# Memory attention in one transformer layer: the query and output weights multiplied into keys and values ahead of time

## The chip, the cores and the metric

The kernel runs on one core of one Trainium2 chip. A core has a matrix engine (TensorE, PE in the profile; PEld is its weight load), a vector engine (DVE), a scalar engine (ACT), a general engine (GpSimd, POOL) and an engine that here only issues transfers (SyncE, SP). Each takes its instructions in order and waits for others by semaphores. Matmuls write to PSUM, which the other engines read; the working memory of 128 partitions is SBUF; main memory (HBM, "DRAM" in the code) is reached by DMA. All DMAs of this kernel are issued from SP's one queue, in order.

The metric is the device time of one launch in microseconds. Three runs of the kernel before gave 1541.18, 1542.2 and 1542.79; the median is 1542.2.

## The reference

One layer of a streaming encoder on x of 1024 rows by 1024 columns, with 256 memory rows. The part that the change touches is the second sub-layer:

```python
def memory_cross_attention(h, mem_n, w_mq, w_mk, w_mv, w_mo):
    q = (h @ w_mq).reshape(B, S, MEM_HEADS, MEM_HEAD_DIM)        # 4 heads of 256
    k = (mem_n @ w_mk).reshape(B, M, MEM_HEADS, MEM_HEAD_DIM)    # M = 256 memory rows
    v = (mem_n @ w_mv).reshape(B, M, MEM_HEADS, MEM_HEAD_DIM)
    logits = jnp.einsum('bshd,bmhd->bhsm', q, k).astype(jnp.float32) * (MEM_HEAD_DIM ** -0.5)
    p = jax.nn.softmax(logits, axis=-1).astype(v.dtype)
    o = jnp.einsum('bhsm,bmhd->bshd', p, v).reshape(B, S, D_MODEL)
    return o @ w_mo

# in reference(), after the token mixing has given x:
h = rmsnorm(x, g_mem_pre[l])
mem_n = rmsnorm(mem, g_mem_kv[l])
y = memory_cross_attention(h, mem_n, w_mq[l], w_mk[l], w_mv[l], w_mo[l])
x = x + rmsnorm(y, g_mem_post[l])
h = rmsnorm(x, g_ff_pre[l])
y = jnp.square(jax.nn.relu(h @ w_ff1[l])) @ w_ff2[l]
```

Ahead of it stand two attentions over x (eight heads each: one with forget gates, one over chunks) with an output projection w_out; behind it stands the MLP. Each sub-layer has a norm before and after it.

## The kernel before

All products are kept near fp32. Each operand is split into a high part that TensorE takes (fp32r) and a low part, the rest. One product is then three matmuls: `mm3` (L100) issues high by high (L102), high by low (L103) and low by high (L104). A weight is loaded as 128 x 1024 numbers (512 KB) by `load_w` (L83) into a raw buffer `wraw`, of which there are three. ACT copies it to the high part `whi` (L96), and DVE or POOL subtracts that for the low part `wlo` (L97), two buffers of each. `lo_eng` (L423) gives the subtraction to DVE and POOL by turns in the first phase, and to DVE alone once `quiet` is set after it. Other tiles of 4 KB a partition (activations, row results) come from one pool `u4` of 31 buffers. PSUM has four tags of two banks each: mm, s, tr and pv.

*First phase (up to about 566 us).* Projections and the attention heads alternate; each head writes its output to main memory (`od`, L393). The normalised memory rows are turned (columns of the model on the partitions, `mT`) in `mem_turn`. At the end of the phase `mem_keys` (L431) makes the keys `km`: 8 weights of w_mk, each used by 24 matmuls of 256 columns (matmuls to tiles mk). `mem_values` (L442) makes the values `vm`: 8 weights of w_mv, each used by 12 matmuls of 512 columns (tiles mv). Keys and values stay in SBUF.

*Second phase.* The sequence is half of 512 rows (`th` = 0 or 1) by half. `head_outputs` (L540) loads the attention outputs from `od` into tiles `oin` (L549), splits them into yT_hi (ACT, L552) and yT_lo (DVE, L553) and adds their squares (L556 to L561) for the group norms. `mix_out` (L583) is the output projection (tiles yw): four matmul blocks to a weight, the squares summed by a small product (ssh, L568), the reciprocal root made on DVE and POOL (L569, L570), evictions on ACT for the first group (L605) and DVE for the second (L607). `close_block` (L629) adds the residual row and norms; `turn` (L643) transposes the rows for the next product, h2 for the memory attention and h3 for the MLP.

`cross(th)` (L647) is the memory attention for one half. For each of four heads: two weights of w_mq, each used by 24 matmuls of 512 columns (tiles mq); the query is split into qh and ql; for each block of 128 rows the scores (tiles ms, 256 columns), maximum, exponential, reciprocal, scaling on POOL (L680); transposes (mtr); and the product with the values (tiles mo), split again. `mem_out` (L613) multiplies with w_mo, 8 weights per half, each used by 24 matmuls of 512 columns (tiles ym).

The order of calls: `cross(0)` at L725 with the turns of the second half's h2 between its heads, `mem_out(0)` at L727, `close_block` of half 0, `cross(1)` at L731 with the turn of half 0's result y0 into h3 after its first head, then the POOL sums `xf` of h3's two parts that the MLP's Strassen scheme needs (L855), the first column half of `mem_out(1)` (L857), the loads `wo` of the second column half (L858), and from `residual_in(0)` on an order written out by hand: the second column half of `mem_out(1)` block by block, between its blocks the residual rows, then the MLP. Up to there the framework's scheduler orders the calls' instructions by its own model of their times; each engine then runs the given order.

Of the kernel before, what the change touches and what calls it, by code (L numbers as in the profile page):

```python
# [13 lines left out]
F32 = mybir.dt.float32  # L14
# [30 lines left out]
def build(ctx, tc, nc, out, t):  # L45
# [122 lines left out]
    cd = dr.tile([8, S], F32, name="cd")  # L168

# [261 lines left out]
    def mem_keys(mT):  # L431
        km = Act("km", NM)
        for nb in range(KC):
            wh, wl = load_w(t["w_mk"][nb], [P, KC, P], lo_on=lo_eng())
            ps = mm_tile([P, NM], f"mk{nb}")
            for kc in range(KC):
                mm3(ps, wh[:, kc, :], wl[:, kc, :], mT.hi(kc), mT.lo(kc), kc == 0, kc == KC - 1)
            nc.scalar.activation(km.hi(nb), ps, AF.Copy)
            nc.vector.tensor_sub(km.lo(nb), ps, f(km.hi(nb)))
        return km  # L440

    def mem_values(mT):  # L442
        vh = [u4(f"vm_hi{m}", (P, D)) for m in range(2)]
        vl = [u4(f"vm_lo{m}", (P, D)) for m in range(2)]
        for nh in range(2):
            cs = slice(nh * HT, (nh + 1) * HT)
            ps = [mm_tile([P, HT], f"mv{nh}{m}") for m in range(2)]
            for kp in range(4):
                wh, wl = load_w(row_pair(t["w_mv"], kp, nh), [P, 2, HT], lo_on=lo_eng())
                for m in range(2):  # L450
                    ms = slice(m * P, (m + 1) * P)
                    for j in range(2):
                        kc = kp * 2 + j
                        mm3(ps[m], mT.hi(kc, ms), mT.lo(kc, ms), wh[:, j, :], wl[:, j, :],
                            kc == 0, kc == KC - 1)
            for m in range(2):
                nc.scalar.activation(vh[m][:, cs], ps[m], AF.Copy)
                nc.vector.tensor_sub(vl[m][:, cs], ps[m], f(vh[m][:, cs]))
        return vh, vl
# [69 lines left out]
    km = mem_keys(mT)  # L529
    vmh, vml = mem_values(mT)  # L530
# [82 lines left out]
    def mem_out(th, o, y, ss, g, nhs=(0, 1)):  # L613

        for nh in nhs:
            cs = slice(nh * HT, (nh + 1) * HT)
            ps = [mm_tile([P, HT], f"ym{th}{nh}{b}", "mm" if b < 2 else "s") for b in range(4)]
            for kp in range(4):
                wh, wl = load_w(row_pair(t["w_mo"], kp, nh), [P, 2, HT], lo_on=lo_eng())
                for b in range(4):  # L620
                    c = slice(b * P, (b + 1) * P)
                    for j in range(2):
                        mm3(ps[b], o[kp][0][:, j, c], o[kp][1][:, j, c], wh[:, j, :], wl[:, j, :],
                            kp == 0 and j == 0, kp == 3 and j == 1)
# [22 lines left out]
    def cross(th, act, after=None):  # L647

        out_h = []
        for h in range(4):  # L650
            qh, ql = [], []
            for nb in range(2):
                wh, wl = load_w(t["w_mq"][h * 2 + nb], [P, KC, P], lo_on=lo_eng())
                ps = mm_tile([P, HT], f"mq{th}{h}{nb}")
                for kc in range(KC):
                    mm3(ps, wh[:, kc, :], wl[:, kc, :], act.hi(kc), act.lo(kc), kc == 0, kc == KC - 1)
                a = p2x.tile([P, HT], F32R, tag="qh", bufs=4, name=f"qh{th}{h}{nb}")
                b = p2x.tile([P, HT], F32R, tag="ql", bufs=4, name=f"ql{th}{h}{nb}")
                nc.scalar.activation(a, ps, AF.Copy, scale=0.0625)
                nc.vector.scalar_tensor_tensor(b, ps, 0.0625, f(a), op0=ALU.mult, op1=ALU.subtract)  # L660
                qh.append(a)
                ql.append(b)
            ph = p2x.tile([P, 2, HT], F32R, tag="ph2", bufs=1, name=f"ph{th}{h}")
            pl = p2x.tile([P, 2, HT], F32R, tag="pl2", bufs=1, name=f"pl{th}{h}")
            for b2 in range(2):
                tr = mm_tile([P, 2, 2, P], f"mtr{th}{h}{b2}", "tr")
                for j in range(2):
                    b = b2 * 2 + j
                    bs = slice(b * P, (b + 1) * P)
                    ps = mm_tile([P, NM], f"ms{th}{h}{b}", "s")  # L670
                    for nb in range(2):
                        mm3(ps, qh[nb][:, bs], ql[nb][:, bs], km.hi(h * 2 + nb), km.lo(h * 2 + nb),
                            nb == 0, nb == 1)
                    st = small.tile([P, 3], F32, tag="mst", bufs=4, name=f"mst{th}{h}{b}")
                    pr = p2x.tile([P, NM], F32, tag="mp", bufs=4, name=f"mp{th}{h}{b}")
                    nc.vector.tensor_reduce(st[:, 0:1], ps, axis=mybir.AxisListType.X, op=ALU.max,
                                            negate=True)
# [3 lines left out]
                    for m in range(2):  # L681
                        nc.tensor.transpose(tr[:, m, j, :], pr[:, m * P:(m + 1) * P], ident)
# [707 lines left out]
```

## Time and profile before

The profiled execution took 1547.0 us; its span, from the first to the last instruction, is 1545.2 us at a mean granted clock of 0.995. What is told below of places in time is counted from the start of that span.

| stretch of the span, us | what TensorE does there | PE busy, us |
|---|---|---|
| 0 to 486 | projections, attention | 467.20 of 486 |
| 486 to 528 | attention and memory keys (mk) | 41.90 of 42 |
| 528 to 566 | attention and memory values (mv) | 36.87 of 38 |
| 566 to 668 | output projection (yw), rest of attention | 98.70 of 102 |
| 668 to 741 | memory attention, half 0 | 67.01 of 73 |
| 741 to 796 | mem_out, half 0 | 55.00 of 55 |
| 796 to 893 | memory attention, half 1; first columns of mem_out | 95.85 of 97 |
| 893 to 960 | rest of mem_out, MLP begins | 62.12 of 67 |
| 960 to 1545.2 | MLP | the rest |

A row of instructions in the profile gives line, engine, operation, result and operands by the program's names, the shape and the count; then durations (ns, least, median, most) and the first and last start, or the busy time and the mean. An idle time is put down to what ended it ("<-").

### The profile page before, as it was taken

Reading aid. Unit: us, or ns where it says so; the run is one execution under the profiler, and the core shown is the slowest. Engines: PE = TensorE matmul, PEld = TensorE weight load, DVE = VectorE, ACT = ScalarE, POOL = GpSimd, SP = SyncE. Lnnn points to the kernel's source line nnn. Section 1 sums busy time; section 2 is a strip of 40 time slices with the busy share of each in tenths; the row PEclk is TensorE's granted clock in tenths of the full one; section 3 lists DMA queues with packets and bytes.
Section 4 is the critical chain, followed back from the end, with each engine's and each line's share of the span. In section 5 each row is a group of like instructions: output and inputs, shape, how many; then the busy total and the mean of one; then the engine's idle time right before and its main releaser. Section 6 shows DMA issues by size and latency. Waiting matters only on the chain. (4 is left out here: it accounts for less than half of the span.)

```text
span 1545.2 us, 21983 instructions
## 1 busy us (share of the span) xinstructions
PE 1501.4 (97%) x7852; PEld 1270.6 (82%) x7852; DVE 938.2 (61%) x1640; ACT 789.8 (51%) x1405; POOL 374.2 (24%) x546
## 2 busy tenths in 40 slices
PE   8999999999999999989999998999999999999998
PEld 7978889789878987768888877888888888888886
DVE  6366574665466773775455468676455574746577
ACT  5356564565466675444444455555555544444442
POOL 4234351343234430121011320443233000000021
PEclk9999999999999999999999999999999999999999
DMA  5132140252222454453143154775444595535565
GB/s 215 50 95 66 52 113 23 66 156 64 56 65 90 121 169 139 160 184 106 55 154 105 55 177 168 242 246 181 153 155 150 189 384 194 171 114 192 198 245 191
DMA packets 83856, 220.71 MB, mean 143 GB/s; under 512 B 9865, under 2 KB 13969, under 8 KB 83746
## 3 DMA queue, kind: packets, MB, share of 16 engines
q1 hardware_dynamic: 83746, 219.30, 42.7%
q8 instruction: 62, 1.02, 0.3%
q14 instruction: 48, 0.39, 0.1%
HBM read 159.96 MB, written 50.91 MB: 136 GB/s over the span
## 5 line engine op out<-in xcount | busy, mean ns | idle before, releaser
L96 ACT ACTIVATE whi<-wraw 128x1024 fp32r<-128x1024 f32 x76 | 80.3, 1058 | 76.5 <-PE ym L104 19.0
L1117 ACT ACTIVATE whif<-ra 128x1024 fp32r<-128x1024 f32 x37 | 39.2, 1061 | 122.1 <-PE fy L103 62.6
L1119 DVE TENSOR_TENSOR wlof<-ra,whif 128x1024 fp32r<-128x1024 f32 x37 | 45.3, 1225 | 91.1 <-ACT whif L1117 91.1
L97 DVE TENSOR_TENSOR wlo<-wraw,whi 128x1024 fp32r<-128x1024 f32 x52 | 63.6, 1225 | 53.8 <-ACT whi L96 53.2
L1233 POOL TENSOR_SCALAR rf<-sf 128x1 f32<-128x1 f32 x8 | 8.3, 1035 | 326.5 <-ACT jf L1218 326.2
L102 PE MATMUL v<-whiv,hT_hi 128*128 128x256 f32 (+1 forms) x256 | 73.6, 287 | 1.0 <-DVE vs L235 1.0
L103 PE MATMUL v<-wlov,hT_hi 128*128 128x256 f32 (+1 forms) x256 | 73.2, 286 | 0.0
L104 PE MATMUL v<-whiv,hT_lo 128*128 128x256 f32 (+1 forms) x256 | 73.1, 286 | 0.0
L97 POOL TENSOR_TENSOR wlo<-wraw,whi 128x1024 fp32r<-128x1024 f32 x24 | 57.8, 2410 | 54.2 <-ACT whi L96 28.1
L102 PE MATMUL fx<-vhif,whif 128*128 128x512 f32 x168 | 65.4, 389 | 0.0
L104 PE MATMUL fx<-vhif,wlof 128*128 128x512 f32 x168 | 65.4, 389 | 0.0
L103 PE MATMUL fx<-vlof,whif 128*128 128x512 f32 x168 | 65.4, 389 | 0.0
L1007 POOL TENSOR_TENSOR sc<-wf,wf 128x512 f32<-128x512 f32 x14 | 22.8, 1627 | 144.4 <-DMA wf<-in_w_ff 125.0
L102 PE MATMUL yw<-whi,yT_hi 128*128 128x512 f32 x128 | 51.0, 403 | 2.2 <-ACT yw L605 1.6
L103 PE MATMUL ym<-wlo,oT_hi 128*128 128x512 f32 x128 | 50.9, 397 | 0.9 <-DVE wlo L97 0.8
L103 PE MATMUL mq<-h2T_lo,whi 128*128 128x512 f32 x128 | 51.5, 402 | 0.0
L102 PE MATMUL mq<-h2T_hi,whi 128*128 128x512 f32 x128 | 51.3, 402 | 0.1
L104 PE MATMUL mq<-h2T_hi,wlo 128*128 128x512 f32 x128 | 51.0, 399 | 0.0
L103 PE MATMUL yw<-wlo,yT_hi 128*128 128x512 f32 x128 | 50.6, 395 | 0.1
L102 PEld LDWEIGHTS v<-whiv,hT_hi 128*128 128x128 f32 x256 | 49.1, 192 | 1.5 <-DVE vs L235 1.2
L104 PE MATMUL yw<-whi,yT_lo 128*128 128x512 f32 x128 | 50.3, 393 | 0.0
L104 PE MATMUL ym<-whi,oT_lo 128*128 128x512 f32 x128 | 50.2, 395 | 0.0
(751 smaller groups left out, 5135.5 us busy)
## 6 DMA issues: line engine op xcount, KB each, us to landing
ra<-gd SPq DMA_DIRECT2D x56, 512.0 KB, 3.8
wg<-in_w_ff SPq DMA_DIRECT2D x56, 512.0 KB, 5.6
wf<-in_w_ff SPq DMA_DIRECT2D x38, 512.0 KB, 3.8
gd<-s SPq DMA_DIRECT2D x48, 256.0 KB, 2.1
wraw<-in_w_qk SPq DMA_DIRECT2D x16, 512.0 KB, 4.0
wraw<-in_w_mq SPq DMA_DIRECT2D x16, 512.0 KB, 4.3
wraw<-in_w_mo SPq DMA_DIRECT2D x16, 512.0 KB, 3.8
gd<-u SPq DMA_DIRECT2D x32, 256.0 KB, 2.1
```

The lines of the kernel that those rows point to most:

```text
L96: nc.scalar.activation(hi, raw, AF.Copy)
L97: (lo_on or nc.gpsimd).tensor_sub(lo, raw, f(hi))
L102: nc.tensor.matmul(ps, lh, rh, start=start, stop=False, skip_group_check=more)
L103: nc.tensor.matmul(ps, lh, rl, start=False, stop=False, skip_group_check=more)
L104: nc.tensor.matmul(ps, ll, rh, start=False, stop=stop, skip_group_check=more)
L1007: eng.tensor_sub(sc[:, k1], r0[:, k0], r1[:, k0])
L1117: nc.scalar.activation(ah, ra, AF.Copy)
L1119: nc.vector.tensor_sub(al, ra, f(ah))
L1233: nc.gpsimd.tensor_scalar(r, ssf[b][:, 0:1], ssf[b][:, 1:2], EPS, op0=ALU.add, op1=ALU.add)
```

## The change

The memory attention is regrouped. Before, (h w_mq) k^T p-softmax, times v, times w_mo. After, for each head h the product w_mq k^T (1024 columns of the model by 256 memory rows, scaled by 1/16) and the product v w_mo (256 memory rows by 1024 columns) are made once, at the end of the first phase, and stored to main memory (`kd_d`, `vd_d`, 2 x 4 tiles of 512 KB each). The four heads' folded keys lie side by side as a weight of 1024 by 1024, and so do the folded values.

- `mem_side` makes both keys and values transposed (256 columns a matmul, 24 matmuls a weight). For the values this takes the place of 12 matmuls of 512 columns a weight.
- `fold_keys`: 8 weights of w_mq^T, each used by 24 matmuls of 256 columns; each result is evicted by ACT or DVE into a u4 tile and stored (16 stores of 256 KB).
- `fold_values`: 8 weights of w_mo, each used by 12 matmuls of 512 columns; 8 stores of 512 KB.
- `cross` loads 8 folded key weights per half (as w_mq was before) and makes the scores of two heads and 128 rows in one bank, four banks at a time. There are no queries, no split of them and no product with the values; the transposed probabilities are split at once and are what `mem_out` multiplies.
- `mem_out` loads the folded values in place of w_mo; the squares of a bank are summed before the bank is scaled.
- The order: `cross(1)` follows `cross(0)` at once, ahead of `mem_out(0)`. The second half's h2 is turned in one go after the first two heads of `cross(0)`. The turn of y0 into h3 moves into the first column half of `mem_out(1)`, after its second and third weights, and the loads `wo` go after its fourth. The sums `xf` follow that `mem_out`.
- The host lays w_mq out transposed and w_mv in column blocks.

```diff
+    kd_d = [[dr.tile([P, 2, HT], F32, name=f"wk{kp}_{nh}") for nh in range(2)] for kp in range(4)]
+    vd_d = [[dr.tile([P, 2, HT], F32, name=f"wv{kp}_{nh}") for nh in range(2)] for kp in range(4)]
...
-    def mem_keys(mT):
...
+    def mem_side(mT, src, name):
+        act = Act(name, NM)
         for nb in range(KC):
+            wh, wl = load_w(t[src][nb], [P, KC, P], lo_on=lo_eng())
+            ps = mm_tile([P, NM], f"m{name}{nb}")
             for kc in range(KC):
                 mm3(ps, wh[:, kc, :], wl[:, kc, :], mT.hi(kc), mT.lo(kc), kc == 0, kc == KC - 1)
+            nc.scalar.activation(act.hi(nb), ps, AF.Copy)
+            nc.vector.tensor_sub(act.lo(nb), ps, f(act.hi(nb)))
+        return act
+
+    def fold_keys(km):
+        for h in range(4):
+            for mh in range(2):
+                wh, wl = load_w(row_pair(t["w_mqT"], h, mh), [P, 2, HT], lo_on=lo_eng())
+                for kp in range(2):
+                    ps = mm_tile([P, 2, NM], f"fk{h}{mh}{kp}")
+                    for a in range(2):
+                        c = slice((kp * 2 + a) * P, (kp * 2 + a + 1) * P)
+                        for d in range(2):
+                            mm3(ps[:, a, :], wh[:, d, c], wl[:, d, c], km.hi(h * 2 + d), km.lo(h * 2 + d),
+                                d == 0, d == 1)
+                    g = u4(f"fks{h}{mh}{kp}", (P, 2, NM), F32)
+                    if kp:
+                        nc.vector.tensor_scalar(g, ps, 0.0625, None, op0=ALU.mult)
+                    else:
+                        nc.scalar.activation(g, ps, AF.Copy, scale=0.0625)
+                    nc.sync.dma_start(kd_d[mh * 2 + kp][h // 2][:, :, h % 2 * NM:(h % 2 + 1) * NM], g)
...
-    def mem_values(mT):
...
+    def fold_values(vm):
         for nh in range(2):
+            for h in range(4):
+                wh, wl = load_w(row_pair(t["w_mo"], h, nh), [P, 2, HT], lo_on=lo_eng())
+                g = u4(f"fvs{h}{nh}", (P, 2, HT), F32)
                 for m in range(2):
+                    ps = mm_tile([P, HT], f"fv{h}{nh}{m}")
                     ms = slice(m * P, (m + 1) * P)
+                    for d in range(2):
+                        mm3(ps, vm.hi(h * 2 + d, ms), vm.lo(h * 2 + d, ms), wh[:, d, :], wl[:, d, :],
+                            d == 0, d == 1)
+                    if m:
+                        nc.vector.tensor_copy(g[:, m, :], ps)
+                    else:
+                        nc.scalar.activation(g[:, m, :], ps, AF.Copy)
+                nc.sync.dma_start(vd_d[h][nh], g)
...
-    km = mem_keys(mT)
-    vmh, vml = mem_values(mT)
+    fold_keys(mem_side(mT, "w_mk", "km"))
+    fold_values(mem_side(mT, "w_mv", "vm"))
     p1s.close()
...
+    def mem_out(th, o, y, ss, g, nhs=(0, 1), hook=lambda kp: None):
...
-                wh, wl = load_w(row_pair(t["w_mo"], kp, nh), [P, 2, HT], lo_on=lo_eng())
+                wh, wl = load_w(vd_d[kp][nh], [P, 2, HT], lo_on=lo_eng())
                 for b in range(4):
                     for j in range(2):
+                        mm3(ps[b], *o_at(o, b, kp * 2 + j), wh[:, j, :], wl[:, j, :],
                             kp == 0 and j == 0, kp == 3 and j == 1)
+                hook(kp)
             for b in range(4):
+                square_sum(ps[b], ss[b][:, nh:nh + 1], HT)
                 nc.vector.tensor_tensor(y[b][:, cs], ps[b], g[:, cs], op=ALU.mult)
-                square_sum(ps[b], ss[b][:, nh:nh + 1], HT)
...
     def cross(th, act, after=None):
...
+        o = []
+        for nh in range(2):
+            ps = [mm_tile([P, HT], f"ms{th}{nh}{b}", "mm" if b < 2 else "s") for b in range(4)]
+            for kp in range(4):
+                wh, wl = load_w(kd_d[kp][nh], [P, 2, HT], lo_on=lo_eng())
+                for b in range(4):
+                    c = slice(b * P, (b + 1) * P)
+                    for j in range(2):
+                        mm3(ps[b], act.hi(kp * 2 + j, c), act.lo(kp * 2 + j, c), wh[:, j, :], wl[:, j, :],
+                            kp == 0 and j == 0, kp == 3 and j == 1)
...
+            for b in range(4):
...
+                nc.vector.tensor_reduce(st[:, 0:2], sc, axis=mybir.AxisListType.X, op=ALU.max, negate=True)
+                for h in range(2):
+                    nc.scalar.activation(pr[:, h, :], sc[:, h, :], AF.Exp, bias=st[:, h:h + 1],
+                                         accum_out=st[:, 2 + h:3 + h])
+                nc.vector.reciprocal(st[:, 4:6], st[:, 2:4])
...
+                    nc.gpsimd.tensor_scalar(pr[:, h, :], pr[:, h, :], st[:, 4 + h:5 + h], 1.0,
+                                            op0=ALU.mult, op1=ALU.mult)
                     for m in range(2):
+                        nc.tensor.transpose(tr[:, h * 2 + m, :], pr[:, h, m * P:(m + 1) * P], ident)
...
-    o = cross(0, h2[0], after={0: turn_mixed(1, PAIRS[:1]), 1: turn_mixed(1, PAIRS[1:])})
+    o = cross(0, h2[0], after={0: turn_mixed(1)})
+    o1 = cross(1, h2[1])
     y, ss = y_tiles("m", 0)
     mem_out(0, o, y, ss, gmpost)
     close_block(y, ss, 0, lambda b: x1d[b], lambda b: x2d[b], gffpre, "h3", range(4))
     h3 = [Act("h3T0")]
-    y0 = y
-    o = cross(1, h2[1], after={0: lambda: turn(y0, 0, h3[0], "h3")})
+    y0, o = y, o1
...
+    def meanwhile(kp):
+        if kp in (1, 2):
+            turn(y0, 0, h3[0], "h3", PAIRS[kp - 1:kp])
+        elif kp == 3:
+            wo.extend(load_w(vd_d[k][1], [P, 2, HT], u4, lo_eng()) for k in range(4))
+
+    mem_out(1, o, y, ss, gmpost, (0,), meanwhile)
     for i in range(4):
         for a in range(2):
             xf[i, a] = pr.tile([P, HT], F32, tag="xf", bufs=8, name=f"xf{i}{a}")
...
-    mem_out(1, o, y, ss, gmpost, (0,))
-    wo = [load_w(row_pair(t["w_mo"], kp, 1), [P, 2, HT], u4, lo_eng()) for kp in range(4)]
...
-        "w_mq": blocks(i["w_mq"][0]),
+        "w_mqT": a(i["w_mq"][0].T),
...
-        "w_mv": i["w_mv"][0],
+        "w_mv": blocks(i["w_mv"][0]),
```

The program after, instruction by instruction, has TensorE go through the key fold between the last attention heads, then through 24 matmuls of the key fold, the values' projection and the value fold with no attention work between them, and then to the output projection. In SP's order the load of the first `oin` stands behind two stores of the value fold and one load of a w_out weight.

More of the change, by code (lines that the diff above doesn't have):

```diff
@@ L696, in cross @@
[L696 to L699 removed]
+            if after and nh in after:
+                after[nh]()
+        return o
     gpost = gain(p2, t["g_mix_post"], "g_mix_post")
```

89 lines of the change are left out of this document (15 added, 74 removed).

## The prediction

> **What bounds the kernel now.** I read the page's first part, then the granted clock, then TensorE's waits by releaser, then busy time by stage. The clock, beside the span:
>
> ```profile
> core 0: 1545.2 us, clock 0.995
> ```
>
> No throttle is in play. The first part of the page gives each engine's busy time and share of the span:
>
> ```profile
> PE 1501.4 (97%) x7852; PEld 1270.6 (82%) x7852; DVE 938.2 (61%) x1640; ACT 789.8 (51%) x1405; POOL 374.2 (24%) x546
> ```
>
> TensorE is the bound: 43.8 us of the 1545.2 are not matmuls. An edit here pays by fewer matmul columns or fewer waits of PE. The waits of PE from 560 to 900 us, the stretch the change rewrites (total, times, longest, in us):
>
> ```profile
> PE ms L104 <- DVE h2y L109: 4.2, 1, 4.2
> PE tr_h L127 <- DVE h2T_lo L141: 2.4, 3, 1.4
> PE yw L102 <- ACT yw L605: 1.6, 3, 0.8
> PE ym L102 <- ACT whi L96: 1.1, 1, 1.1
> PE ym L103 <- DVE wlo L97: 0.8, 1, 0.8
> ...
> PE yw L102 <- DVE yw L607: 0.6, 1, 0.6
> ```
>
> Nothing else in 340 us is above .7. Busy time by stage (stretch; its length; busy time and instructions of PE, PEld, DVE, ACT, POOL; granted clock, DMA share, GB/s):
>
> ```profile
> 528.00:566.00 38.00, 36.87 (x214) 32.02 (x213) 29.83 (x65) 29.95 (x55) 17.67 (x30) 1.00 0.56 174
> 668.00:741.00 73.00, 67.01 (x338) 56.09 (x338) 42.60 (x73) 31.53 (x68) 13.78 (x27) 0.95 0.39 124
> 741.00:796.00 55.00, 55.00 (x264) 45.77 (x264) 23.80 (x37) 20.59 (x40) 3.21 (x7) 1.00 0.24 77
> 796.00:893.00 97.00, 95.85 (x497) 81.01 (x496) 54.50 (x92) 46.09 (x95) 25.74 (x38) 1.00 0.30 98
> 1235.00:1275.00 40.00, 39.28 (x174) 32.20 (x173) 31.03 (x29) 18.72 (x20) 0.00 (x0) 1.00 0.99 383
> ```
>
> In the first, memory values (mv) are mixed with the last attention work. The next three are the cross-attentions of both halves and the first mem_out: the second cross is full but for 1.15 us, the mem_out has no gap at all. The last row, in the MLP, is the fullest DMA stretch.
>
> **Change, part 1: matmul columns.** A matmul is issued every so many us; first and last of 22 consecutive ones of 256 columns, and of 18 of 512:
>
> ```profile
> 499.58 0.28 PE L102 MATMUL mk<-mT_hi,whi 128*128 128x256 f32 x1
> ...
> 502.09 0.28 PE L102 MATMUL mk<-mT_hi,whi 128*128 128x256 f32 x1
> ...
> 796.01 0.39 PE L102 MATMUL mq<-h2T_hi,whi 128*128 128x512 f32 x1
> ...
> 799.86 0.39 PE L104 MATMUL mq<-h2T_hi,wlo 128*128 128x512 f32 x1
> ```
>
> 2.51/21 = .1195 us and 3.85/17 = .2265 us. Folding keys costs 192 matmuls of 256 columns, and the old scores were 192 of 256. Folding values costs 96 of 512, and the old value products mo were 96 of 512. The new scores (2 halves x 2 x 4 weights x 24 of 512) equal the old mq, 384. So the fold removes no work; it moves it. Only the values' projection alters shape, 96 of 512 to 192 of 256: 192 x .1195 - 96 x .2265 = **+1.2**. The removed evictions of q and o are worth 0: PE was busy 55.00 of 55.00 and 95.85 of 97 beside them.
>
> **Part 2: splits ahead of PE.** Each weight takes an ACT copy (whi), then a subtraction (wlo) on DVE or POOL by turns:
>
> ```profile
> L96 ACT ACTIVATE whi<-wraw x76: 1037/1061/1076, 59.2 to 898.0; 128x1024 fp32r<-128x1024 f32 x76
> L97 DVE TENSOR_TENSOR wlo<-wraw,whi x52: 1211/1226/1306, 445.6 to 899.1; 128x1024 fp32r<-128x1024 f32 x52
> L97 POOL TENSOR_TENSOR wlo<-wraw,whi x24: 2382/2398/2655, 60.4 to 558.6; 128x1024 fp32r<-128x1024 f32 x24
> ```
>
> From the chain of waits, the cost of handing over (matmul, copy, subtraction, matmul):
>
> ```profile
> 951.40 0.24 PE py L104
> 951.66 1.05 ACT whi_a L792
> 952.74 1.24 DVE wlo_a L795
> 954.02 0.50 PE px L104
> ```
>
> Hand-overs take .02 to .05. With two buffers a copy can begin when the weight two back is used up, so on POOL wlo stands .02 + 1.06 + .03 + 2.40 + .05 = 3.56 after that. In the new order the key fold fills the attention's tail, where the mv stood, and what follows is about 47 us of mv (24 matmuls a weight) and value fold (12 a weight) with nothing between. Cover for a mv weight: 24 x .1195 + 2 matmuls not needing wlo, 3.11: a stall of .45, four times. For a value-fold weight: 12 x .2265 plus one or two matmuls: .61 once, .39 three times. Together **+3.6**; the four each on DVE (2.39) fit. Ends 0 (POOL quicker than inferred, or old attention work left in the stretch) and 3.6. I take the upper: each duration has a row.
>
> **Part 3: transfers of the fold.** 16 more loads of 512 KB and 24 stores, 16.8 MB, all on SP's queue. The value fold moves 1.05 MB (load, store) per 3.17 us (12 x .2265 + .45) = 331 GB/s; rows above stand at 174 GB/s for a share of .56 (311 at 1.0) and 383 at .99. So it lies between just too much and enough: 0 to 2.6 (8 x 1.05 MB at 311 against 331, 1.6, and 1 for the loads at the head of mv). I take **+1.0**.
>
> **Part 4: the hand-over to the output projection (yw).** Before, its inputs were loaded from 545.6 while attention and mv ran; the tile oin:
>
> ```profile
> L549 SPq DMA_DIRECT2D oin<-od x16: 320/436/811, 545.6 to 605.4; - x16
> L552 ACT ACTIVATE yT_hi<-oin,gcol x16: 708/722/727, 550.8 to 608.4; 128x512 fp32r<-128x512 f32 x16
> ...
> L559 ACT ACTIVATE oin<-oin x4: 1042/1061/1062, 558.5 to 610.5; 128x1024 f32<-128x1024 f32 x4
> L560 DVE TENSOR_TENSOR sq<-sq,oin x4: 691/693/1853, 559.6 to 611.6; 128x512 f32<-128x512 f32 x4
> ...
> DMA to landing us min/median/max: 2.7/4.4/9.2
> ```
>
> On SP's queue these loads now stand behind two stores of the value fold and behind the load of the first output weight, which waits for a raw buffer, that is for POOL's split of the eighth and last mo weight, which follows once the sixth is used up. Call the last fold matmul F. The sixth mo weight is used up at F - 24 x .2265 = F - 5.4; + 3.56 frees the buffer at F - 1.9, the first oin is issued about F - 1.1, lands 4.4 later (2.7 to 9.2), + .72 for yT_hi: PE starts at F + 4.0. Its 12 matmuls last 2.7; the second oin waits behind another weight (copy 1.06, split 1.23), is issued near F + 3.6 and ready at F + 8.7: 2.0 more. The squares (.72 + 1.06 + two of .69) make the row sums late by .5. Then ACT has four yT_hi and two squares of the other half ahead of the first eviction, and the reciprocal root needs POOL:
>
> ```profile
> L570 POOL TENSOR_TENSOR rs<-rs,mhalf 128x4 f32<-128x4 f32 x4 | 4.5, 1126 | 48.7 <-DVE rs L569 48.7
> ```
>
> First eviction F + 15.2, PE at its wait F + 12.4: 2.8. Sum 4.0 + 2.0 + .5 + 2.8 = **+9.3** (2.3 to 14.1, by the landing's ends and by whether the later steps hide). The waits of yw on evictions which this absorbs, 1.6 + .6: **-2.2**.
>
> **Part 5: the cross.** The wait of 4.2 for old scores (ql queued on DVE behind a step that waited for a late x row) goes with ql; the longest transpose wait, 1.4, gets 12 score matmuls in front: **-5.6**. New: scores in groups of four banks; the next group's bank needs a maximum and two exponentials, 18 matmuls (4.1 us) cover that, not always: **+1.0** (0 to 3). cross(1) before mem_out(0) covers the softmax end of both.
>
> **Part 6: tail.** The waits of ym for whi and wlo, 1.1 + .8, go with the new order. The turn of y0 into h3 now sits inside the second mem_out. Its rows:
>
> ```profile
> L641 DVE SCALAR_TENSOR_TENSOR ym<-xth,h3x,g_ff_pre x4: 1283/1285/1285, 800.8 to 817.1; 128x1024 f32<-128x1024 f32 x4
> ```
>
> The last is ready 817.1 + 1.3 - 796.0 = 22.4 after the first mem_out ends; PE reaches its turn after 96 matmuls, 21.7: +1. The POOL sums of h3 slide to just before the MLP's first rows:
>
> ```profile
> L855 POOL TENSOR_TENSOR xf<-h3T_hi,h3T_lo 128x512 f32<-128x512 f32 x8 | 10.1, 1297 | 8.2 <-PE mo L104 8.2
> ```
>
> 8 x 1.3 = 10.4 ahead of POOL's steps for the rows: 0 to 3, taken 0, since 96 matmuls of the last ym (21.7) lie beside them. In all **-.9** (-1.9 to +2.1).
>
> **Sum.** 1.2 + 3.6 + 1.0 + 9.3 - 2.2 - 5.6 + 1.0 - .9 = +7.4. The profiled run took 1547.0 (span 1545.2), so 1554.4 there; it lies .3% above the median 1542.2 of the runs, and median with median gives **1549.6**. All terms at their low ends: 1.2 + 2.3 - 2.2 - 5.6 - 1.9 = -6.2, 1536.0; all high: 1.2 + 3.6 + 2.6 + 14.1 - 2.2 - 5.6 + 3 + 2.1 = +18.8, 1561.0.
>
> **Rivals.** *Other side: the hand-over hides.* If the output weight's raw buffer frees in time, oin lands in 2.7 and splits and stores stay beside PE, only the low ends remain: 1536.0. It decides once stalls of splits, transfers and hand-over together are under 3.4 (they are 13.9 in the forecast; 3.4 less the forecast's other terms' -6.5 is -3.1). For it: before, the loads were issued from 545.6, while the fold's place was still mv. Against: the queue order after, in which they stand behind the fold's last load and stores.
> *Waits only move.* The waits taken out of the cross come back one for one elsewhere, leaving the columns: 1543.5. For it: stages with PE 55.00 of 55.00 had none to give. Against: two of the waits have a cause that is deleted.
> *DMA-bound fold.* At the longest landing (9.2 for 4.4, +4.8) and 311 GB/s in the value fold (+1.6) beside the forecast's terms: +13.8, 1556.0. For it: .56 for 174. Against: 383 reached elsewhere.
> *Two vector engines in each other's way.* Two rows side by side:
>
> ```profile
> 558.56 2.39 POOL L97 TENSOR_TENSOR wlo<-wraw,whi 128x1024 fp32r<-128x1024 f32 x1 [4.65 <-DVE yT_lo L553]
> 559.64 1.85 DVE L560 TENSOR_TENSOR sq<-sq,oin 128x512 f32<-128x512 f32 x1 [1.13 <-ACT oin L559]
> ```
>
> The sum on DVE took 1.85, not its median .69, and ended within .6 us of POOL's split end. If each of 8 pairs of splits in the fold ran one after the other, PE would lose a DVE split each beside the forecast's terms: 8 x 1.23 = 9.8, 1559.4. Against: a DVE split starts 3.97 after its pair's buffer is free, POOL's ends at 3.56. [...]
>
> **How the numbers follow.** Forecast .44 (own range 1545.5 to 1556), DMA-bound .17, engines blocking .04: slower, .65. Waits only move, .13: within .2% (3.1 us, about what a measurement of this kernel can tell from no change). Hidden hand-over, .22: faster. The range 1536 to 1561 is that of the bounds: under 2 in 10 lie outside.
>
> **What would show it.** Part 1: mv with 192 matmuls at .12. Part 2: PE waiting about .4 for wlo from POOL, up to eight times. Part 3: DMA share near 1 in the fold. Part 4: one wait of PE of 3 to 5 us for yT_hi of the first output products, then smaller ones for yT, rs and yw, all within 16 us; oin issued after the last fold loads. Part 5: no ms wait over 1; stretches of cross with PE full. Part 6: no xf or row step in PE's chain. Wrong I would be if oin's issue lies 5 us or more before the last fold matmul, or if PE stays busy across the hand-over.

## The result, and the profile after

The changed kernel took 1562.5 us (median of 4 runs, 1561.18 to 1563.93) against 1541.7 for the kernel before (1539.35 to 1542.79): 1.0137 of it, 95% interval 1.0120 to 1.0155, or +20.8 us. The forecast had +7.4 and a range that ended at 1561.0. The direction was right; the size was not.

The first part of the page of the kernel after, in the form shown for before:

```profile
PE 1509.3 (97%) x7948; PEld 1279.5 (82%) x7948; DVE 937.0 (60%) x1604; ACT 798.0 (51%) x1409; POOL 398.5 (26%) x554
```

The span is 1560.3 at a mean clock of .990 (before .995). The waits of PE in the rewritten stretch, 525 to 960 us (total, times, longest):

```profile
PE yw L102 <- ACT yT_hi L574: 6.2, 2, 5.7
PE yw L102 <- ACT yw L627: 4.4, 4, 2.5
PE tr_h L127 <- DVE h3T_lo L141: 3.7, 2, 2.4
PE mvm L104 <- POOL wlo L97: 1.9, 4, 0.6
PE fv L102 <- DVE fvs L478: 1.7, 3, 0.6
PE ssh L590 <- DVE sq L583: 1.5, 1, 1.5
PE ym L102 <- DVE h3T_lo L141: 1.1, 1, 1.1
```

Four places: the hand-over to the output projection (yw, ssh), the values' projection (mvm) and value fold (fv), and the turn of y0 in the last mem_out (tr_h, ym). Busy time by stage, with the granted clock as the third number from the end:

```profile
594.00:625.00 31.00, 23.69 (x98) 17.52 (x97) 11.99 (x14) 14.83 (x19) 9.54 (x4) 0.99 0.87 289
625.00:630.50 5.50, 4.97 (x12) 3.80 (x12) 2.11 (x3) 2.27 (x4) 0.00 (x0) 0.50 1.04 398
639.60:645.00 5.40, 5.35 (x13) 4.24 (x14) 1.38 (x2) 1.52 (x2) 0.00 (x0) 0.50 0.00 0
645.00:733.00 88.00, 85.54 (x389) 69.19 (x388) 51.70 (x68) 44.41 (x73) 10.74 (x19) 1.00 0.40 132
733.00:833.00 100.00, 99.00 (x482) 81.43 (x481) 60.61 (x90) 50.69 (x115) 24.00 (x42) 1.00 0.41 137
833.00:893.00 60.00, 60.00 (x278) 49.66 (x277) 29.16 (x37) 24.58 (x46) 9.30 (x18) 1.00 0.37 127
893.00:934.00 41.00, 36.16 (x158) 29.13 (x158) 31.14 (x30) 20.07 (x36) 24.02 (x24) 0.92 0.58 200
910.50:915.00 4.50, 4.50 (x12) 3.54 (x12) 4.50 (x7) 2.14 (x3) 4.50 (x4) 0.53 0.64 225
```

The crosses (733 to 833) and the first 60 us behind them are full. But PE is "busy" in rows two, three and eight at a clock of .50 to .53 (the last row lies inside the one above it): each follows a wait of 2.4 us or more, and 12 or 13 matmuls take the time of 20 to 24 at full clock. The page counts that as work, so the waits alone do not tell the loss.

To see all of it, take for each matmul of the trace the time to the next start less its issue pace (.227 us for 512 columns, .12 for 256, .11 for 128; the few other widths by their own usual pace). The sum is what PE lost, waits and slow matmuls together. Against a second profile of the kernel before (first experiment, span 1539.1, thus 21.2 less):

| stretch | before, lost | after, lost | difference |
|---|---|---|---|
| start to the memory keys | 38.3 | 38.2 | -.1 |
| keys, values (and fold) up to the last | 2.4 | 8.4 | +6.0 |
| hand-over and output projection, to the first product of the cross | 5.7 | 20.9 | +15.2 |
| both crosses, both mem_outs | 11.3 | 10.6 | -.7 |
| MLP | 5.7 | 5.0 | -.7 |
| issue pace of all matmuls | 1465.9 | 1467.1 | +1.2 |

What is left to the two spans, some 10 us in each, lies ahead of the first matmul and behind the last. Nearly three quarters of the loss stand at the hand-over. Columns of matmul cost what was reckoned, 1.2.

### The profile page after: what moved, and what is told of

Read it like the earlier page. It is cut to its first block, busy times and chain, and to the rows that moved or that the text cites. A ratio compares the mean times of both kernels' runs of the same rounds, so it can differ in the third digit from the quotient of the medians.

```text
span 1560.3 us, 22213 instructions
## 1 busy us (share of the span) xinstructions
PE 1509.3 (97%) x7948; PEld 1279.5 (82%) x7948; DVE 937.0 (60%) x1604; ACT 798.0 (51%) x1409; POOL 398.5 (26%) x554
## 4 chain that ended last, share of the span: by engine, by line
PE 84%; DVE 5%; ACT 4%; issue 3%; DMA 2%; POOL 2%; SPq 0%; DVEq 0%; POOLq 0%; ACTq 0%
PE fx L103 4%; PE fx L104 3%; PE fx L102 3%; PE fy L102 3%; PE fy L104 3%; PE fy L103 3%; PE px L104 3%; PE px L102 3%; PE px L103 3%; PE v L102 2%; PE v L104 2%; PE v L103 2%; PE ym L102 2%; PE ym L103 2%; PE ym L104 2%
## 5 line engine op out<-in xcount | busy, mean ns | idle before, releaser
L96 ACT ACTIVATE whi<-wraw 128x1024 fp32r<-128x1024 f32 x92 | 97.3, 1059 | 110.9 <-PE ym L104 24.9
L97 DVE TENSOR_TENSOR wlo<-wraw,whi 128x1024 fp32r<-128x1024 f32 x60 | 75.4, 1259 | 77.2 <-ACT whi L96 76.9
L1133 ACT ACTIVATE whif<-ra 128x1024 fp32r<-128x1024 f32 x37 | 39.2, 1060 | 121.8 <-PE fy L103 62.6
L97 POOL TENSOR_TENSOR wlo<-wraw,whi 128x1024 fp32r<-128x1024 f32 x32 | 76.9, 2403 | 82.9 <-ACT whi L96 62.2
L103 PE MATMUL ms<-wlo,h2T_hi 128*128 128x512 f32 x128 | 50.2, 392 | 0.0
L104 PE MATMUL ms<-whi,h2T_lo 128*128 128x512 f32 x128 | 50.1, 396 | 0.0
L104 PEld LDWEIGHTS v<-whiv,hT_lo 128*128 128x128 f32 x256 | 49.5, 193 | 0.4 <-DVE hT_lo L141 0.2
```

The source lines that it names most:

```text
L96: nc.scalar.activation(hi, raw, AF.Copy)
L97: (lo_on or nc.gpsimd).tensor_sub(lo, raw, f(hi))
L103: nc.tensor.matmul(ps, lh, rl, start=False, stop=False, skip_group_check=more)
L104: nc.tensor.matmul(ps, ll, rh, start=False, stop=stop, skip_group_check=more)
L1133: nc.scalar.activation(ah, ra, AF.Copy)
```

## The experiments

**The kernel before once more.** The kernel is the same.

> The kernel before, unchanged, for a second profile of it. Theory A: the wait of 4.2 us of PE for the old scores (behind a late x row), and the 12 matmuls at half pace that follow it (12 x 0.2 = 2.4 us), belong to the one profiled execution; then this profile has no wait over 2 us there and its span is 4 to 7 us under 1545.2. Theory B: the wait is in every run; then it stands again at 3 us or more and the profile again lies about 0.3% above the median.

Measured: .9997 of before (.9987 to 1.0007); the profiled execution took 1540.85, its span 1539.1. Its waits of PE from 560 to 900:

```profile
PE tr_h L127 <- DVE h2T_lo L141: 2.4, 3, 1.4
PE yw L102 <- ACT yw L605: 1.8, 3, 1.2
PE ym L102 <- ACT whi L96: 1.6, 2, 1.1
PE ym L103 <- DVE wlo L97: 1.5, 2, 0.8
PE pvc7g L387 <- DVE plc7g L381: 1.4, 1, 1.4
PE ms L104 <- DVE h2y L109: 0.7, 1, 0.7
```

The 4.2 for the old scores are .7 here. The wait behind the late x row and the 12 slow matmuls after it (2.4) make most of the 6.1 us between the two spans. Theory A holds by both of its signs: the forecast booked a saving that one profile of the same kernel has and the other has not. How many of the other runs have it is not known; their median, 1543.7, lies between the two profiled times.

**Three single edits of the change**, on one chip. First, the splits of the value side on DVE:

```diff
     fold_keys(mem_side(mT, "w_mk", "km"))
+    quiet[0] = True
     fold_values(mem_side(mT, "w_mv", "vm"))
```

> After the change, with the low parts of all w_mv and w_mo weights of the fold made on DVE. Theory A (POOL's 2.40 us split is what PE waits for): the four waits of 0.6 for POOL's wlo go, 2 to 3 us faster than the change. Rival (DVE is short there): the evictions of the fold queue behind the splits on DVE, the waits for fvs grow by as much, no gain (within 1 us).

Measured: 1.0098 (1.0083 to 1.0114). The waits for POOL's wlo are gone, and those for fvs fell to .9; the two stretches of mvm and fv take 49.7 us, not 52.7. A wait of 1.4 for whi came. Theory A, by the waits and the stretch; in time 4 to 6 us (against 1.0122 and 1.0137, the change's two measurements), more than its 2 to 3, though the intervals don't rule 3 out.

Second, the inputs of the output projection ahead of the value fold:

```diff
-    fold_values(mem_side(mT, "w_mv", "vm"))
+    vm = mem_side(mT, "w_mv", "vm")
     ...
     parts = {(th, 0): head_outputs(th, 0) for th in range(2)}
+    fold_values(vm)
```

> After the change, with the first group's head outputs called ahead of the value fold, so that their loads stand ahead of its loads and stores on SP's queue. Theory A (the hand-over to yw stalls because of the queue order): the waits of yw for yT_hi (5.7 and 0.5), of ssh for sq (1.5) and of the first eviction (2.5) go together with the matmuls at half pace, 10 to 13 us faster than the change. Rival (the fold's transfers fill the DMA engines): the fold itself then stalls, and the gain is under 4 us.

Measured: 1.0070 (1.0055 to 1.0085), 8 to 10 us of the 19 to 21 back: the low end of theory A or just under it. The waits at the hand-over went, so the queue order did cost them. But the row-sum product moved into the fold and waited there, and the clock fell behind it (waits of PE; busy time by stage):

```profile
PE ssh L589 <- DVE sq L582: 3.4, 1, 3.4
PE yw L102 <- ACT yw L626: 1.8, 3, 0.8
PE fv L102 <- ACT fvs L480: 1.4, 1, 1.4
```
```profile
602.50:610.00 7.50, 5.74 (x18) 4.79 (x19) 6.18 (x10) 4.94 (x8) 1.47 (x1) 0.55 0.47 178
```

The mvm and fv stretch grew from 52.7 to 62.6, while hand-over and output projection shrank from 113.7 to 96.3.

Third, the calls of before in their order:

```diff
     o = cross(0, h2[0], after={0: turn_mixed(1)})
-    o1 = cross(1, h2[1])
     y, ss = y_tiles("m", 0)
     mem_out(0, o, y, ss, gmpost)
     ...
-    y0, o = y, o1
+    y0 = y
+    o = cross(1, h2[1], after={0: lambda: turn(y0, 0, h3[0], "h3")})
```

> After the change, with the calls of before in their order: cross(0), mem_out(0), cross(1) with the turn of y0 in it, the xf sums, then mem_out(1). Theory A (the turn of y0 inside the last mem_out is what costs the tail 7 to 8 us): the waits of tr_h and ym for h3T_lo go, 5 to 8 us faster than the change. Rival (the order of cross and mem_out is worth something): new waits for softmax and transposes in the crosses, 1 to 3 us each, take the gain back, within 2 us of the change.

Measured: 1.0098 (1.0083 to 1.0113), 4 to 6 us faster than the change. No wait for h3T_lo; in its place, between 780 and 960:

```profile
PE px L104 <- DVE wlo_a L806: 2.2, 1, 2.2
PE ym L102 <- ACT oT_hi L706: 2.0, 2, 1.2
```

Theory A: the change's order of calls costs more than it hides.

**What makes the tail's wait?** Three kernels with the change's own order. Both pairs of the turn behind the last weight; the POOL sums replaced; the last four weights (wo) taken early:

```diff
 turn_late:  -  if kp in (1, 2): turn(..., PAIRS[kp - 1:kp])   elif kp == 3: wo.extend(...)
             +  if kp == 3: wo.extend(...); turn(y0, 0, h3[0], "h3")
 xf_light:   -  nc.gpsimd.tensor_add(xf, h3 high, h3 low)
             +  nc.scalar.activation(xf, h3 high, AF.Copy)
 wo_early:   -  elif kp == 3: wo.extend(...)
             +  elif kp == 0: wo.extend(...)
```

The kernel xf_light leaves the low part out of the sums; it asks only what they cost.

> After the change, with both pairs of the turn of y0 called after the fourth weight of the second half's mem_out and behind the splits of the last four weights. Theory A (PE reaches the turn ahead of the rows): the waits for h3T_lo (3.7 and 1.1) go, 4 to 7 us faster than the change. Rival (the four splits on DVE are what delays h3T_lo): the waits stay or grow, within 2 us of the change.

> After the change, with the eight xf sums of POOL replaced by eight copies of h3's high part on ACT; the low part is left out of xf. Theory A (POOL's sums and DVE's splits hold each other up): the four splits of DVE in the turn take 1.23 us each and not 1.7 to 2.25, the waits for h3T_lo fall by about 2 us, 2 to 4 us faster. Rival (the splits delay h3T_lo by their number alone): the waits stay at 4.8 within 0.7, no gain over 1 us.

> After the change, with the loads and splits of the last four folded weights (wo) called after the first weight of the last mem_out and not after its fourth, so that their splits don't stand among the turn's evictions. Theory A (these splits, queued among the evictions on ACT and DVE, make the waits for h3T_lo): the waits of 3.7 and 1.1 fall under 2 in sum, 3 to 6 us faster than the change. Rival (the rows are late): the waits stay, within 1.5 us of the change.

First the change itself. Its last row was ready 22.7 us after the last matmul of mem_out(0) (878.6 to 901.3), and PE came to the last transposes behind that, at 902.3. What it then waited for were the turn's evictions h3T_lo, each of which stands behind a split wlo on DVE:

```profile
900.03 1.28 DVE L669 SCALAR_TENSOR_TENSOR ym<-xth,h3x,g_ff_pre 128x1024 f32<-128x1024 f32 x1 [1.77 <-POOL h3x L112]
902.93 1.23 DVE L97 TENSOR_TENSOR wlo<-wraw,whi 128x1024 fp32r<-128x1024 f32 x1
904.08 0.68 DVE L141 TENSOR_TENSOR h3T_lo<-tr_h,h3T_hi 128x512 fp32r<-128x512 f32 x1
904.94 2.25 DVE L97 TENSOR_TENSOR wlo<-wraw,whi 128x1024 fp32r<-128x1024 f32 x1 [0.18 <-ACT whi L96]
907.11 0.68 DVE L141 TENSOR_TENSOR h3T_lo<-tr_h,h3T_hi 128x512 fp32r<-128x512 f32 x1
907.71 1.69 DVE L97 TENSOR_TENSOR wlo<-wraw,whi 128x1024 fp32r<-128x1024 f32 x1
909.32 0.68 DVE L141 TENSOR_TENSOR h3T_lo<-tr_h,h3T_hi 128x512 fp32r<-128x512 f32 x1
```

PE went on at 904.8, 907.8 and 910.1, each time as an h3T_lo ended.

Measured: 1.0163, 1.0110, 1.0136 (intervals of ±.002). The waits of the three, in this order, beside 3.7 and 1.1 in the change (turn_late, xf_light, wo_early):

```profile
PE tr_h L127 <- DVE h3T_lo L141: 6.7, 2, 3.7
PE ym L102 <- DVE h3T_lo L141: 2.4, 1, 2.4
```
```profile
PE tr_h L127 <- DVE h3T_lo L141: 2.7, 2, 1.4
PE ym L102 <- DVE h3T_lo L141: 2.2, 1, 2.2
```
```profile
PE tr_h L127 <- DVE h3T_lo L141: 6.1, 2, 4.4
PE ym L102 <- DVE h3T_lo L141: 2.4, 1, 2.4
```

No single edit takes the wait away, and by the waits the rival holds in all three. Turning later made it worse (by more than the rival's 2 us), so PE isn't merely ahead of the rows; without the POOL sums 4.9 stay of 4.8; with the four splits out of the way the row chain itself got later (the last row's DVE step starts at 906.2, in the change at 900.0, and the row is ready 27.2 us after mem_out(0) and not 22.7). Rows, splits and turn share ACT and DVE in some 25 us; that whatever goes first delays the rest is a reading of the three together, which no run shows by itself. (xf_light was 2 to 4 us faster than the change all the same; 2.4 of them lie behind the last matmul of mem_out, 624.0 us to the end and not 626.4.) Only more time between mem_out(0) and the turn, as in the kernel with the old order, was seen to take the wait away.

One effect showed cleanly on the way. Beside POOL's sums, a DVE split took 2.25 in the change (the row at 904.94 above), and the sums 7.91/4 = 1.98 each (1.30 in the profile of before); without the sums the same split took 1.23, as did the change's split at 902.93, ahead of them. The first row is the change's, the second xf_light's:

```profile
904.84 7.91 POOL L874 TENSOR_TENSOR xf<-h3T_hi,h3T_lo 128x512 f32<-128x512 f32 x4 [4.84 <-DVE h3T_lo L141]
```
```profile
905.74 1.23 DVE L97 TENSOR_TENSOR wlo<-wraw,whi 128x1024 fp32r<-128x1024 f32 x1 [0.18 <-ACT whi L96]
```

This did not make the tail's wait: it was 4.9 without the sums.

**The half clock.** Twenty extra matmuls in the long wait:

```diff
     fold_values(vm)
+    warm = mm_tile([P, HT], "warm")
+    for n in range(20):
+        nc.tensor.matmul(warm, vm.hi(n % 8, ...), vm.h[n % 2] ..., start=n == 0, stop=n == 19)
```

> After the change, with 20 extra matmuls of 512 columns (4.5 us; their sums go nowhere) behind the last value-fold matmul, inside the wait for yT_hi. Theory A (a long wait of PE is followed by some 5 us at half clock, whatever comes next): the first output products run at 0.227 us and not 0.426, 2 to 3 us faster than the change though PE has more to do. Rival (these matmuls are slow because their operands come slowly): they stay at 0.426, no gain.

> The changed kernel, unchanged, on the chip of the three beside it: 1.012 to 1.0155 of before; waits and half-clock stretches as in its first profile, within 1 us each.

Measured: 1.0128 (1.0112 to 1.0145) beside 1.0122 (1.0106 to 1.0138) for the change again, on one chip: no gain in sum. But the clock did what theory A says. In the filled place, and behind the unfilled wait of 2.5 that follows:

```profile
629.50:634.50 5.00, 3.29 (x12) 2.10 (x12) 2.11 (x3) 2.32 (x5) 0.00 (x0) 1.00 1.04 406
643.00:648.00 5.00, 5.00 (x15) 4.02 (x16) 1.38 (x2) 1.87 (x3) 0.00 (x0) 0.67 0.01 3
```

The first output products ran at full clock (1.00, one started every .23 us, where the change had .50 and .426); PE then came sooner to the next missing input (the second wait for yT_hi was 1.9, .5 before). Also, a wait for whi in the values' projection happened to be 2.3 and not 1.2, as it is in the change run again, and the fold ended 2.0 us later than there (623.3 for 621.3). So at this place the slow matmuls went with PE's idleness ahead of them, not with their operands; curing them alone saved nothing here, and how much of that was the later fold and how much the late inputs behind is not shown.

**Head outputs earlier still.** Four kernels call them ahead of the values' projection, with the splits of it and of the fold on DVE:

```diff
-    fold_values(mem_side(mT, "w_mv", "vm"))
     ...
     parts = {(th, 0): head_outputs(th, 0) for th in range(2)}
+    fold_values(mem_side(mT, "w_mv", "vm"))
 best1: with the turn as in turn_late      best2: with the calls in the order of before
 best3, best4: ssh in the PSUM tag mm; best3 with the order of before, best4 with the change's
```

> After the change, with the head outputs ahead of the values' projection and value fold, the low parts of those weights on DVE, and the turn of y0 as in turn_late. Theory A (stalls of the hand-over, the fold and the tail make all of the loss beside the 1.2 us of matmul issue): between 2 us faster than before and 4 us slower. Rival (the waits move on): 8 us or more slower than before.

> As best1, but with the calls of cross and mem_out in the order of before and the turn of y0 in the second cross. Theory A: between 2 us faster than before and 5 us slower, waits for oT_hi of 1 us at the ends of the two crosses. Rival (the waits move on): 8 us or more slower than before.

> As best2 (head outputs first, fold splits on DVE, calls in the order of before), with the product of the row sums (ssh) in the PSUM tag mm, so that it can't stand in the middle of the values' projection. Theory A (the fold itself costs only 1.2 us of issue; all else was stalls and the half clock behind them): no wait over 2.5 us from 560 to 760, within 4 us of before either way. Rival (the fold displaces work that nothing hides): 8 us or more slower than before, in new waits.

> As best3, but with the change's own order of calls and its turn of y0 in the last mem_out. Theory A: slower than best3 by the tail alone, that is by the waits for h3T_lo (4.8) and about 2 us of half clock, 5 to 8 us less the waits for oT_hi (2): 3 to 7 us slower than best3. Rival (the tail's waits come from the late hand-over): within 2 us of best3.

Measured: 1.0145, 1.0103, 1.0143, 1.0158; best4 is 2.5 us behind best3, under its 3 to 7. All theories of gain fell: the wait went into the values' projection, whole (in best1 and best2 it is the product ssh that waits there, 16.6 and 17.9 us). From best3, a wait of PE, then ACT and DVE:

```profile
PE mvm L102 <- DVE vm_lo L443: 20.6, 1, 20.6
```
```profile
584.91 1.40 ACT L573 ACTIVATE yT_hi<-oin,gcol 128x512 fp32r<-128x512 f32 x2 [7.92 <-DMA oin<-od]
```
```profile
592.82 0.75 DVE L443 TENSOR_TENSOR vm_lo<-mvm,vm_hi 128x256 fp32r<-128x256 f32 x2
```

ACT stood 7.9 us at a head output whose transfer was late, and the split of the next weight and the eviction vm_lo stood behind the whole group of head outputs in ACT's and DVE's order. The scheduler puts these instructions where it believes their data to be there.

**The edits together, and an order written out.** combo puts the three single edits together (with ssh in mm). manual writes out the order of projection, fold and head outputs: loads first, weights split two ahead, head outputs as pieces between late weights. It also gives the split weights of the fold buffers out of the pool u4 in place of two of each, makes all their low parts on DVE, and has the calls in the order of before. manual_new is manual with the change's order of calls. The code is shortened:

```diff
+    with tc.manual_schedule():
+        for n in range(16):                  # 8 weights of w_mv, 8 of w_mo
+            load(n + 3); split(n + 2)        # low part on DVE
+            ... matmuls, evictions, store of weight n ...
+            pieces of the head outputs after n = 1, 4 (loads), 9, 11, 13, 14 (splits, squares)
```

> After the change, with the values' projection, the value fold and the first group's head outputs in an order written out: loads of the inputs of the output projection early on SP, their work on ACT and DVE between the last weights of the fold, weights split three ahead on DVE; cross and mem_out called in the order of before. Theory A (the fold itself costs 1.2 us of matmul issue, the rest of the loss is waits that an order can avoid): no wait over 2 us from 560 to 740, no stretch at half clock there, 1.5 to 5 us slower than before or level. Rival (ACT, DVE or the DMA engines have no room for the fold beside PE): waits of 8 us or more remain in sum there, 8 us or more slower than before.

> As the kernel beside it, with the change's own calls (both crosses first, the turn of y0 in the last mem_out). Theory A (the tail costs by itself, whatever stands ahead of it): 4 to 8 us slower than the one beside it, waits for h3T_lo of 4 to 6 us and some 10 matmuls at half clock behind them. Rival (the tail's waits follow from the late hand-over): within 2 us.

> After the change, with the three single edits together and no written order: head outputs called between the values' projection and the value fold, all low parts of both on DVE, calls in the order of before, row-sum product in the PSUM tag mm. Theory A (the gains of the single edits, 10.3, 6 and 6 us of 21, add up, as they act at different places): within 3 us of before. Rival (the waits of one come back in the next, as in the kernels with the head outputs ahead of the projection): 6 us or more slower than before.

Measured: manual 1.0061 (1.0048 to 1.0074), manual_new 1.0080 (1.0066 to 1.0094), combo 1.0061 (1.0045 to 1.0076). By the numbers given ahead, the rival in both: nearly half of the loss is left. In manual it stands as waits for evictions of the fold (fvs, 8.0 in five and two waits) behind head-output work on ACT; in combo the gains did not add up. manual_new is 3 us slower than manual, a little under its 4 to 8, and its waits for h3T_lo are 3.7 and 1.6: the tail costs by itself.

manual2 gives the fold twice the banks and spreads the pieces:

```diff
-    ps = mm_tile([P, HT], f"fv{h}{nh}{m}")
+    ps = mm_tile([P, HT], f"fv{h}{nh}{m}", ("mm", "s")[m])    # mvm: by n % 2
+    loads of oin after n = 2, 3, 4, 6; one split and square after each of n = 5..10, 12, 13
```

> As manual, with twice the PSUM banks for the values' projection and value fold (tags mm and s by turns), the loads of the head outputs one tile at a time and their work in eight pieces spread over the weights. Theory A (what is left in manual are evictions of the fold behind other ACT work, and weight loads behind a burst of other loads, some 13 us with the half clock): the waits for fvs (8.0) and vm_lo (2.1) go, 5 to 9 us faster than manual, within 4 us of before. Rival (ACT and DVE are full there): the waits only change their names, within 3 us of manual.

Measured: 1.0043 (1.0028 to 1.0058), 3 us from manual. The waits for fvs went and waits for wlov (3.7) and whiv (3.0) came: the rival so far. In it ACT stood up to 1.9 us at a square in place, waiting for DVE to have read the same tile. manual3 takes that out of ACT's way:

```diff
+    split(n + 2); load(n + 5)        # first in each step
+    square of a piece one step after its yT_hi and yT_lo
```

> As manual2, with the split of the weight after next first in each step, weight loads five ahead, and the squares of the head outputs one step behind their splits, so that ACT does not wait for DVE in the middle of the fold. Theory A (the 12 us of small waits left in the fold are order): the waits for wlov and whiv in the value fold (6.7) fall under 2, 4 to 8 us faster than manual2, from 1 faster to 3 us slower than before. Rival (ACT and DVE have no room): within 2 us of manual2.

Measured: .9982 of before (.9972 to .9992; 1540.5 against 1543.9, 11 and 14 runs), some 3 us faster than before, more than its theory had, and the fastest of all here. Its waits of PE from 525 to 760, and two stages:

```profile
PE mvm L104 <- DVE wlov L97: 2.1, 2, 1.3
PE yw L102 <- ACT yw L706: 2.0, 3, 1.0
PE mtr L782 <- POOL mp L779: 0.6, 1, 0.6
```
```profile
567.00:616.00 49.00, 46.30 (x295) 41.85 (x295) 36.37 (x47) 32.30 (x48) 1.47 (x1) 1.00 0.94 327
616.00:713.00 97.00, 94.36 (x427) 76.17 (x426) 54.16 (x72) 46.76 (x78) 10.74 (x19) 1.00 0.45 152
```

The same loads, stores, splits and matmuls as in the change, with PE 46.3 of 49 and the clock at 1.00; DMA share .94. ACT, DVE and the queue have the room, so the rival is refuted. From manual2 to manual3 the edit is order alone, and 9 us went. The whole way from the change took more than order: the buffers out of u4, twice the banks, the low parts on DVE and the calls of before are in it, and their shares were not told apart. Nor does a profile show where the 3 us against before come from: the spans of this one and of the second profile of before are 1539.2 and 1539.1.

## Why the prediction was wrong

It was right that the fold only moves matmul work (+1.2, and 1.2 was measured), that the hand-over is the largest cost, and in what order its waits stand. By its parts:

- *Part 1, columns:* right.
- *Part 2, splits (+3.6), and part 3, transfers (+1.0):* the sum 4.6 stands against +6.0. For mvm the waits for POOL's split were .4 to .6, as reckoned. In the value fold PE didn't wait for POOL but for DVE's eviction fvs, three times .6, which the forecast had not seen; DVE and POOL both had a share. Late loads showed only through the splits: the wait of .8 for DVE's wlo in mvm stands behind a copy whi that had waited 2.2 for its weight; from 594 to 625 the queue moved 289 GB/s.
- *Part 4, hand-over (+9.3, less 2.2):* this is the step that failed most. Its waits were 5.7, .5, 1.5 and 2.5, 10.2 in all, for 4.0, 2.0, .5 and 2.8: sound. The second difference is the clock: two stretches at .50, in each of which some 5 us of matmuls lost about 2.5 us, were put at nothing. The forecast had read the mean clock of .995 as "no throttle is in play", though its own row 668 to 741 (.95) holds the same thing behind the 4.2 us wait. The -2.2 was wrong too: the old waits of yw on evictions came again as they were (1.9 of the 4.4, and .5). +15.2 was measured for +7.1.

The loads were late as read from the queue's order, and slower to land than the 4.4 taken (tile oin after: first issue 617.9, first split 624.8):

```profile
L571 SPq DMA_DIRECT2D oin<-od x16: 319/426/812, 617.9 to 664.6; - x16
L574 ACT ACTIVATE yT_hi<-oin,gcol x16: 706/714/726, 624.8 to 673.8; 128x512 fp32r<-128x512 f32 x16
...
DMA to landing us min/median/max: 4.5/6.7/8.0
```

- *Part 5, cross (-5.6, +1.0):* the 4.2 stood in the profiled execution of before, which at 1547.0 was 4.8 above the median that the forecast was set against, and is .7 in the second profile. The sum was made on that execution and carried over; the row's count of one wait was the warning.
- *Part 6, tail (-.9):* wrong in sign. The term that was priced held: the last row was ready 22.7 us after mem_out(0)'s end, where 22.4 were taken. The turn's own evictions were put at nothing; they queued on DVE with four splits, 4.8 us of waits, and 2 us of half clock came behind. Parts 5 and 6 together: -5.5 forecast, -.7 measured.

The four differences, +1.4, +8.1, +4.8 and -.7 in the MLP, make the 13.6 between +7.4 and the 21 of the table. The rival nearest in time, two vector engines in each other's way (1559.4), was not what happened: in the fold POOL's splits took 2.38 to 2.40 and DVE's 1.22 to 1.23, their usual times, and no two of them ran side by side. Of the DMA-bound one only part came: the first oin took 6.9 us from issue to split, between the 4.4 of the sum and the 9.2 of the rival, and in the fold a split that had waited for a load cost PE .8. The rival "hidden hand-over" came true only where the order was written out for it, in manual3. The clause on what would prove the forecast wrong (oin issued 5 us before the last fold matmul) did not come to pass: oin was issued 1.7 us ahead of that matmul's end, F = 619.6. The direction came out for the reason given, the late hand-over; the size did not.

## What to carry to other kernels

Work moved out of a loop into one block keeps its instructions and loses its cover: before moving it, list what the engines did beside the old place and what stands behind the new one on each in-order queue. A stall of PE should be priced with the half clock behind it: here, behind the waits of 5.7 and 2.5 us at the hand-over, about 2.5 us more at each of the two places. And a saving that rests on a single wait of one profiled run should be looked for in a second run before it is booked.

## What the runs showed of the hardware

In the change the granted clock fell to .50 at three of the places above, for 6.8 us each: from 624.6, inside the wait of 5.7; from 638.3, inside the wait of 2.5 that came soon after the 1.5 for ssh; from 907.9, as the turn's wait of 2.4 ended, with one of 1.3 ahead of it. In these stretches matmuls of 512 columns started every .426 us (256 columns: .21), behind them every .227. In the profile of before it was .50 from 686.1 to 693.0, around the end of the wait of 4.2 (687.1), and for 3.4 us behind two waits of 1.2 and .8 close together (894.3 to 897.8); a wait of 2.4 for wlo_a that ended at 940.0 had no fall (1.00 from 897.9 to 1000). In oin_early, behind the 3.4 for ssh, it was .50 from 604 to 610, in best2, behind the 17.9, from 590 to 596.

After the wait of 5.7 the matmuls were slow for 5.9 us (625.5 to 631.4), after that of 2.5 for 5.4 (639.7 to 645.1): both times the low clock had begun inside the wait, 4.8 and 1.2 us into it. The first of the two:

```profile
619.60:624.60 5.00, 0.19 (x1) 0.00 (x0) 1.92 (x2) 1.06 (x1) 0.00 (x0) 1.00 0.93 272
628.00:631.40 3.40, 3.02 (x8) 1.82 (x6) 0.32 (x1) 0.66 (x1) 0.00 (x0) 0.50 1.05 393
```

What sets the fall and its length is not shown by these runs.
